# A recurrent and convolutional backbone on one core: the recurrence's GpSimd operations on VectorE

## The chip, the cores and the metric

The kernel runs on one core of a Trainium2 chip. The metric is the device time of one execution in microseconds; the time before is the median of three runs.

## The reference

A stream of 512 latent tokens of width 1024 with 256 context tokens goes through two layers. Layer 0 mixes the tokens with a gated linear recurrence in both directions (8 heads of 128 features, chunks of 64 steps), layer 1 with a short gated convolution; each is followed by a squared-ReLU MLP. All weights are fp32. What matters here is layer 0's recurrence:

```python
def step(s, blk):                       # one chunk of 64 steps
    qb, kb, vb, gb = blk
    cum = jnp.cumsum(gb, axis=2)        # g = log f, f the forget gate, k = 1 - f
    ref = cum[:, :, CHUNK // 2 - 1:CHUNK // 2]
    last = cum[:, :, -1:]
    o_inter = einsum('bhck,bhkv->bhcv', qb * exp(cum), s)
    scores = einsum('bhck,bhsk->bhcs', qb * exp(cum - ref), kb * exp(ref - cum))
    scores = where(lower, scores, 0.0)
    o_intra = einsum('bhcs,bhsv->bhcv', scores, vb)
    s_new = exp(last)[:, :, 0, :, None] * s + einsum('bhsk,bhsv->bhkv', kb * exp(last - cum), vb)
    return s_new, o_inter + o_intra
...
o = o * rsqrt(mean(o * o, axis=-1, keepdims=True) + EPS)      # per head
o = o * gnorm * silu(gate);  y = o.reshape(...) @ w_out
```

Context tokens give only the state from which each direction of the latent scan starts.

## The kernel before, in words

Features lie in partitions, tokens in the free dimension. Every fp32 product of weights and activations is made of three products of a high and a low part: ScalarE casts the high part (`whi`, L316), another engine subtracts it from the fp32 tile for the low part (`wlo`, L317; 128x1024 for half a block of weights). TensorE takes weights high with activations high and low first, and the remaining low part last (L340, L343).

Layer 0 runs head by head, in pairs (`hp`), an even head A and an odd head B. For a head, `logs` (L646) makes the sums of log f on VectorE: minimum (L666), two scans per direction (L671, L672; L678, L680), the difference to the chunk's middle (L685), then the context's part: `gc` (L694), its scan (L697), the keys k (L702), the chunk ends `el` (L705), the context's keys (L709), and at its end the decayed context keys `kc` (L711). ScalarE runs Ln and Exp between them. `latent_ops` (L740) then makes the operands of the latent products for each direction: three products of keys (`kl`, and both halves of d3, L750 to L753), the products with q (L755 to L760). TensorE transposes `kc` (`ctr`, L718), makes the context's state, transposes the keys (`ktr`, L778), and makes the states, the masked scores and the output.

TensorE's queue is in program order, and the order around the recurrence is written out by hand: `Fill` puts as many products of the next block between the recurrence's steps as the table `GAPS` says (for head 7: 30 ahead of `ctr`, 20 behind it). These products are the next head's forget gates (`forget_steps`, whose weights `wf` come in two halves, for heads 1 to 7) and queries, or in head 7 the out projection of heads 0 to 3 (`out_steps`). That one multiplies `y_hi` and `y_lo` of a finished head (`y_split`, L230); for heads 0 to 3 they are traced behind head 7's `latent_ops`, and `h_pair` gives them the slots of the input activations h0, which come free when the last products with h0 are done. `readout` (L829) scales a head's y with gain and gate, then with the reciprocal root (L833).

On the other engines the framework's scheduler sets the order: an engine takes, of the operations whose inputs are ready by the scheduler's reckoning, the one traced first; blocks under `tc.high_priority()` (the weights' parts among them) come ahead of the rest. Once built, each engine runs its queue strictly in order.

Of the kernel before, what the change touches and what calls it, by code (L numbers as in the profile page):

```python
# [13 lines left out]
ALU = mybir.AluOpType  # L14
PSUM = bass.MemoryType.PSUM
DRAM = bass.MemoryType.DRAM
# products between the steps of a head's recurrence: before and behind the context's transposes, behind those of each
# direction's keys (and before its second scores), before the output's products and before its mean square's
# [10 lines left out]
P = 128  # L29
# [17 lines left out]
def dit_kernel(ctx, tc, x, c, ctx_in, c_ctx, ada_w, ada_b, norm1, norm2, norm_f, mlp_w1, mlp_w2,  # L47
# [31 lines left out]
    # ScalarE's functions run in groups that one table set serves; the order of the groups is held.  # L79
# [19 lines left out]
    def dma_w(dst, src):  # L99
        """Weights in the order of their use; the vectors' loads come behind those traced so far."""  # L100
        ins = nc.sync.dma_start(dst, src)
        if weight_dma[0] is not None:
            tc.add_manual_dep(ins.ins, weight_dma[0].ins.name, NOSYNC, reason="load order")
        return ins
# [9 lines left out]
    # ---------------------------------------------------------------- loads of the set-up  # L114
# [12 lines left out]
    def ada_chunk(k):  # L127
        """Columns of feature tile k of the first shift (0..127) and scale (128..255), as two halves over the rows."""
# [27 lines left out]
    # ---------------------------------------------------------------- constants  # L156
# [7 lines left out]
    # adds rows 2, 3 of four to rows 0, 1  # L164
# [25 lines left out]
    # silu(c), silu(c_ctx); feature index p * KT + j  # L190
# [9 lines left out]
    # ---------------------------------------------------------------- norms  # L200
# [4 lines left out]
    def pin(*names):  # L205
        """The order of these operations on their engine."""
        for a, b in zip(names, names[1:]):
            tc.add_manual_dep(pins[b].ins, pins[a].ins.name, NOSYNC, reason="order")

    def rsqrt(v, w, name, n, pool=None):  # L210
        """1 / sqrt(v / n + EPS), with a Newton step behind the tables' values."""
# [14 lines left out]
    def split(t, c0, c1, shift, hi, lo, eng=nc.vector):  # L226
        """hi + lo = t + shift, hi with the bits that a float32r product carries."""
# [14 lines left out]
    # tokens in partitions: 1 / rms of each as a row, alike in all partitions  # L242
# [28 lines left out]
    def first_parts(k):  # L271
        """The parts of the weights' columns behind the shift and scale of feature tile k."""
        raws = ada_raw.get(k) or ada_chunk(k)
        with tc.high_priority():
            ada_parts[k] = [part for h in range(2) for part in split_first(raws[h], f"adst{k}_{h}")]

    def first_rows(k):
        """Rows (products with the parts of c, c_ctx) of the shift and scale of feature tile k."""
# [12 lines left out]
    # ------------------------------------------------- vectors as feature columns  # L291
# [19 lines left out]
    # ---------------------------------------------------------------- weights  # L311
# [8 lines left out]
    def load_half(name, *srcs, **kw):  # L320
        """KH * P rows by CB columns of weights as (hi, lo); the columns may come in pieces."""
# [6 lines left out]
    def load_block(name, *srcs, **kw):  # L328
        """D rows by CB columns, as two halves over the rows."""
        return [load_half(f"{name}_{h}", *(s[h * KH * P:(h + 1) * KH * P, :] for s in srcs), **kw) for h in range(2)]  # L330

    def mm_steps(ps, w, ms, rhs, ks, c0, c1, first, last, fresh=False):
        """The products of the k tiles ks (of one half) in W[:, ms].T @ (hi + lo)[:, c0:c1]; last those of the part
        that comes last: rhs's lo if it is `fresh`, the weights' lo otherwise."""
# [16 lines left out]
    def block_steps(w, pss, rhs):  # L351
        """Both feature tiles of a block, one product at a time."""
# [4 lines left out]
    class Fill:  # L357
        """Products that TensorE runs between the steps of a head's recurrence, while other engines work on these."""
# [4 lines left out]
        def gap(self):  # L363
            """The products that the next wait takes, behind what has come so far."""
# [6 lines left out]
        def step(self, first, last=None):  # L371
            """A step of the recurrence."""
# [4 lines left out]
        def finish(self, i=0):  # L377
            """The rest of the products of the i-th kind."""
# [6 lines left out]
    def block_products(w, rhs, consume, name, c0, c1, m=0, norm=None, parts=0, fresh=False):  # L385
        """Both feature tiles of a block, rows in halves outside. TensorE's part of a `norm` whose sums are still
        on their way comes behind `parts` of the block's products."""
        # a fresh operand's first block does not wait for the banks of the products before it
# [13 lines left out]
    def later(done, c0, c1):  # L402
        """A norm that is due once the products behind it are under way."""
# [3 lines left out]
    def stage(srcs, rhs, consume, name, first=0, last=0, done=None):  # L407
        """All blocks; the first `first` and the last `last` of them together, in halves of the columns.
        `done` is called with each half of the columns that the last blocks have finished."""
# [3 lines left out]
        for gi, g in enumerate(groups):  # L413
            halved = (first > 1 and gi == 0) or (last and gi == len(groups) - 1)
            # behind a norm, VectorE has the norm's work
# [11 lines left out]
    # ---------------------------------------------------------------- adaLN vectors  # L427
# [44 lines left out]
    def ada_finish(ins=None):  # L472
        """The columns of vectors whose rows have come back; behind ins, as the way through DRAM takes its time."""
# [28 lines left out]
    # ---------------------------------------------------------------- first adaLN vectors, h and hc  # L502
# [12 lines left out]
    def first_vectors(k):  # L515
        """shift and scale of feature tile k, for latent and context."""
# [29 lines left out]
    # the first two blocks take the feature tiles as they come  # L546
# [4 lines left out]
    def other_vectors():  # L551
# [5 lines left out]
        # lower bounds: softmax over the layer axis (size N), cumulative sum minus first  # L557
# [72 lines left out]
    # ---------------------------------------------------------------- layer 0: HGRN2  # L630
# [15 lines left out]
    def logs(zs, hd):  # L646
        """Sums of log f. zs: {"c": (z, sigmoid), 0: .., 1: ..}; the operations that ScalarE's Exp waits for first."""
# [14 lines left out]
        for d in range(2):  # L662
            r = R[d]
            z, g, gi, name = r["z"], r["g"], r["gi"], f"{hd}_{d}"
            # the table's logarithm ends at 2^-64; without a lower bound log f is z down there
# [26 lines left out]
        for d in range(2):  # L692
            zd = zc[:, d * CTX:(d + 1) * CTX]
            nc.vector.scalar_tensor_tensor(out=gs[d], in0=zd, scalar=col(lbig, d, hd), in1=gs[d], op0=ALU.add, op1=ALU.min)  # L694
            # the sums over the steps behind each one, one column on from the step's own
# [18 lines left out]
    def context_states(kc, hd, vc, fill):  # L714
        """Both directions' states behind the context; kc = (forward | backward) columns, decayed to the end."""
# [24 lines left out]
    def latent_ops(r, q, d, name):  # L740
        """Operands of the products over pairs of chunks; `f` is the pair's first chunk in this direction."""
# [8 lines left out]
        nc.gpsimd.tensor_tensor(out=v3(kl), in0=v4(kk)[:, :, f, :], in1=v4(d3)[:, :, f, :], op=ALU.mult)  # L750
        nc.gpsimd.tensor_tensor(out=v4(d3)[:, :, 1 - f, :], in0=v4(kk)[:, :, 1 - f, :], in1=v4(d3)[:, :, 1 - f, :],
                                op=ALU.mult)
        nc.gpsimd.tensor_tensor(out=v4(d3)[:, :, f, :], in0=v3(kl), in1=bc(1 - f), op=ALU.mult)  # L753
# [40 lines left out]
    def recurrence(hd, ops, s0, v, fill):  # L794
        """Masked scores, states and o (times QS) of a head; leaves o in yT and its mean square's sums in PSUM."""
# [18 lines left out]
        if hd < HEADS - 1:  # L814
            # the squares in two parts, as the weights are
# [13 lines left out]
    def readout(hd, pr, gate):  # L829
# [3 lines left out]
        (nc.gpsimd if hd < HEADS - 1 else nc.vector).tensor_tensor(out=y, in0=y, in1=r, op=ALU.mult)  # L833

    def silu_part(part, hp, qg):
        def f(m, ps, c0, c1):
            s = ht("qg", f"qg{part}_{hp}_{m}", SEQ, 4)
            act_fn(s, ps, AF.Sigmoid)
            # q, and with it every product up to o, is carried times QS: room for the scores behind the mask
# [5 lines left out]
    def forget_steps(hd, got):  # L845
        got["w"] = w = load_block(f"f{hd}", *fcols(hd), eng=nc.gpsimd)
# [16 lines left out]
    def out_steps():  # L863
        """The out projection of heads 0 .. 3."""
# [42 lines left out]
    for hp in range(4):  # L907
# [41 lines left out]
        if hp == 3:  # L949
            for hd in range(KH):  # L950
                y_split(hd, nc.gpsimd)
# [307 lines left out]
```

## Time and profile before

| | |
|---|---|
| median of 3 runs | 1451.79 us (1449.75 to 1454.37) |
| span of the profiled execution | 1450.0 us |
| TensorE busy | 1383.1 us (95%) |
| VectorE busy | 914.6 us (63%) |
| ScalarE busy | 578.8 us (40%) |
| GpSimd busy | 185.6 us (13%), 160 instructions |
| mean granted TensorE clock | 0.982 |

The recurrence of layer 0 lies between about 80 and 540 us. Engines in the rows: PE is TensorE's products, DVE VectorE, ACT ScalarE, POOL GpSimd. A product's "busy" is modelled, products overlap, and the time from one start to the next is what one costs. An engine's idle time before an instruction stands in brackets with what ended it.

### The profile page before, as it was taken

The page shows a single profiled execution, that of the slowest core. Times are in us where ns is not written, and L with a number is a line of the kernel's source. Part 1 is how long each engine was busy: PE and PEld are TensorE (multiplying, and loading weights), DVE is VectorE, ACT ScalarE, POOL GpSimd, SP SyncE. Part 2 cuts the span into 40 slices and gives each one's busy share as a digit, 9 for nine tenths or more (in the row PEclk, how much of TensorE's full clock was granted, in tenths as well). Part 3 has the DMA queues.
Part 4 walks back from the last instruction along what each step waited for, and adds up shares of the span by engine and source line. Part 5 has one row for each costly group of instructions (what it writes and reads, how often), then busy time and mean ns, then how long its engine had stood idle before and what let it go on. Part 6 is the DMA issues. An engine that isn't in the chain of part 4 may idle for free.

```text
span 1450.0 us, 18678 instructions
## 1 busy us (share of the span) xinstructions
PE 1383.1 (95%) x7418; PEld 1171.7 (81%) x7418; DVE 914.6 (63%) x1305; ACT 578.8 (40%) x877; POOL 185.6 (13%) x160
## 2 busy tenths in 40 slices
PE   6999899989899989999999999999999999999997
PEld 4797787878787779788888888988898788888887
DVE  6695876876776888666566446644467644444436
ACT  6573355445355444233242333322234423232333
POOL 3031232141132130000000003000030100000000
PEclk9999999999999999999999999999999999999999
DMA  9623213333221133775566332332324532332311
GB/s 267 200 59 102 88 45 102 116 93 97 59 74 44 59 131 131 232 218 164 182 190 191 116 92 74 98 102 88 102 91 156 160 102 87 102 102 87 102 58 59
DMA packets 142267, 167.60 MB, mean 116 GB/s; under 512 B 6692, under 2 KB 121572, under 8 KB 142180
## 3 DMA queue, kind: packets, MB, share of 16 engines
q1 hardware_dynamic: 140964, 164.70, 36.4%
q0 software_dynamic: 1088, 1.65, 0.5%
q8 instruction: 58, 0.95, 0.3%
q14 instruction: 29, 0.24, 0.0%
q10 hardware_dynamic: 128, 0.05, 0.0%
HBM read 164.25 MB, written 2.14 MB: 115 GB/s over the span
## 4 chain that ended last, share of the span: by engine, by line
PE 62%; DVE 11%; ACT 2%; DMA 2%; issue 1%; DVEq 0%; SPq 0%; ACTq 0%
PE ps_w L340 20%; PE ps_w L343 10%; PE ps_w2t L1197 4%; PE ps_w2t L1196 4%; PE ps_w2t L1198 4%; DMA ada<-in_ada_w_dram 2%; PE ps_cvb L340 2%; PE ps_cwo L340 2%; PE ps_cvc L340 2%; PE ps_cvx L340 2%; PE ps_fl L340 1%; PE ps_cvb L343 1%; DVE mt_a L1017 1%; PE ps_cwo L343 1%; DVE h_a_lo L233 1%
## 5 line engine op out<-in xcount | busy, mean ns | idle before, releaser
L316 ACT CAST whi_w<-raw_w 128x1024 fp32r<-128x1024 f32 x128 | 134.0, 1052 | 276.7 <-PE ps_w L340 145.5
L317 DVE TENSOR_TENSOR wlo_w<-raw_w,whi_w 128x1024 fp32r<-128x1024 f32 x116 | 141.4, 1222 | 160.5 <-ACT whi_w L316 159.9
L340 PE MATMUL ps_w<-h_a_hi,whi_w 128*128 128x512 f32 (+1 forms) x576 | 208.5, 368 | 2.5 <-ACT h_a_hi L232 2.5
L340 PE MATMUL ps_w<-h_a_lo,whi_w 128*128 128x512 f32 x448 | 174.4, 389 | 0.0
L340 PEld LDWEIGHTS ps_w<-h_a_hi,whi_w 128*128 128x128 f32 x576 | 109.2, 190 | 21.1 <-ACT h_a_hi L232 2.9
L444 DVE SCALAR_TENSOR_TENSOR acc<-ada,cs,acc 128x1024 f32<-128x1024 f32 x70 | 90.6, 1294 | 49.8 <-DMA ada<-in_ada_w_dram 49.7
L343 PE MATMUL ps_w<-h_a_hi,wlo_w 128*128 128x512 f32 x448 | 119.7, 389 | 0.0
L1196 PE MATMUL ps_w2t<-whi_w,u_hi 128*128 128x512 f32 (+1 forms) x288 | 105.4, 366 | 0.0
L1197 PE MATMUL ps_w2t<-wlo_w,u_hi 128*128 128x512 f32 (+1 forms) x288 | 105.4, 366 | 0.0
L1198 PE MATMUL ps_w2t<-whi_w,u_lo 128*128 128x512 f32 (+1 forms) x288 | 105.3, 366 | 0.0
L340 PE MATMUL ps_w<-u_lo,whi_w 128*128 128x512 f32 (+1 forms) x288 | 103.4, 366 | 0.4 <-DVE u_lo L1068 0.4
L340 PE MATMUL ps_w<-u_hi,whi_w 128*128 128x512 f32 (+1 forms) x288 | 103.5, 367 | 0.0
L343 PEld LDWEIGHTS ps_w<-h_a_hi,wlo_w 128*128 128x128 f32 x448 | 84.1, 188 | 17.5
L340 PEld LDWEIGHTS ps_w<-h_a_lo,whi_w 128*128 128x128 f32 x448 | 84.1, 188 | 17.3
L1067 DVE TENSOR_TENSOR mr<-mr 128x512 f32<-128x512 f32 (+1 forms) x72 | 45.0, 629 | 45.6 <-ACT u_hi L1066 45.6
L1065 ACT ACTIVATE mr<-ps_w 128x512 f32<-128x512 f32 (+1 forms) x72 | 39.2, 545 | 81.7 <-PE ps_w L343 81.6
L343 PE MATMUL ps_w<-u_hi,wlo_w 128*128 128x512 f32 (+1 forms) x288 | 70.2, 366 | 0.0
L340 PEld LDWEIGHTS ps_w<-u_lo,whi_w 128*128 128x128 f32 x288 | 54.4, 189 | 9.6 <-DVE u_lo L1068 0.8
L340 PEld LDWEIGHTS ps_w<-u_hi,whi_w 128*128 128x128 f32 x288 | 54.3, 189 | 9.1
L1198 PEld LDWEIGHTS ps_w2t<-whi_w,u_lo 128*128 128x128 f32 x288 | 54.4, 189 | 8.8 <-issue 0.2
L1196 PEld LDWEIGHTS ps_w2t<-whi_w,u_hi 128*128 128x128 f32 x288 | 54.4, 189 | 8.8
L1197 PEld LDWEIGHTS ps_w2t<-wlo_w,u_hi 128*128 128x128 f32 x288 | 54.4, 189 | 8.7
(376 smaller groups left out, 3245.2 us busy)
## 6 DMA issues: line engine op xcount, KB each, us to landing
raw_w<-in_mlp_w_dram SPq DMA_DIRECT2D x128, 512.0 KB, 3.8
ada<-in_ada_w_dram SPq DMA_DIRECT2D x80, 512.0 KB, 4.5
adaw<-in_ada_w_dram SPq DMA_DIRECT2D x32, 256.0 KB, 5.4
raw_f<-in_hgrn_w_in_dram SPq DMA_DIRECT2D x32, 256.0 KB, 3.5
raw_p<-in_hgrn_w_in_dram SPq DMA_DIRECT2D x12, 512.0 KB, 3.5
raw_v<-in_hgrn_w_in_dram SPq DMA_DIRECT2D x8, 512.0 KB, 4.7
raw_cvb<-in_conv_w_in_dram SPq DMA_DIRECT2D x8, 512.0 KB, 3.7
raw_cwo<-in_conv_w_out_dram SPq DMA_DIRECT2D x8, 512.0 KB, 3.5
```

The costliest lines, as they stand in the source:

```text
L233: i1 = nc.vector.scalar_tensor_tensor(out=lo[:, c0:c1], in0=t, scalar=shift, in1=hi[:, c0:c1], op0=ALU.add, op1=ALU.subtract)
L316: pins[name] = nc.scalar.copy(hi, raw)
L317: eng.tensor_tensor(out=lo, in0=raw, in1=hi, op=ALU.subtract)
L340: yield nc.tensor.matmul(ps, lhsT=w[i][:, k % KH, ms], rhs=rhs[k][j][:, c0:c1], start=(k == first and (i, j) == (0, 0)), stop=False)
L343: yield nc.tensor.matmul(ps, lhsT=w[late[0]][:, k % KH, ms], rhs=rhs[k][late[1]][:, c0:c1], start=False, stop=(k == last))
L444: ins = nc.vector.scalar_tensor_tensor(out=acc, in0=raw[:, 0, :], scalar=cs[:, j, 0:1], in1=acc, op0=ALU.mult, op1=ALU.add)
L1017: ins = nc.vector.scalar_tensor_tensor(out=t, in0=xT[k][:, c0:c1], scalar=a[:, k:k + 1], in1=r, op0=ALU.mult, op1=ALU.mult)
L1065: nc.scalar.activation(r, ps, AF.Relu)
L1067: nc.vector.tensor_tensor(out=r, in0=r, in1=r, op=ALU.mult)
L1196: nc.tensor.matmul(ps, lhsT=u[k][0][:, tk], rhs=whi[:, kk, c0:c1], start=(k == 0), stop=False)
L1197: nc.tensor.matmul(ps, lhsT=u[k][0][:, tk], rhs=wlo[:, kk, c0:c1], start=False, stop=False)
L1198: nc.tensor.matmul(ps, lhsT=u[k][1][:, tk], rhs=whi[:, kk, c0:c1], start=False, stop=(k == KT - 1))
```

## The change

Four groups of operations go from GpSimd to VectorE; nothing else changes (the diff also drops comments, which keeps the line numbers). The three key products of `latent_ops` (16 times each), the low parts of the forget weights (two halves for each of heads 1 to 7), the last scaling of y in the readouts of heads 0 to 6, and the low parts of y for heads 0 to 3 (`y_split` without an engine uses VectorE). `GAPS` stays as it is.

```diff
-        nc.gpsimd.tensor_tensor(out=v3(kl), in0=v4(kk)[:, :, f, :], in1=v4(d3)[:, :, f, :], op=ALU.mult)
-        nc.gpsimd.tensor_tensor(out=v4(d3)[:, :, 1 - f, :], in0=v4(kk)[:, :, 1 - f, :], in1=v4(d3)[:, :, 1 - f, :],
+        nc.vector.tensor_tensor(out=v3(kl), in0=v4(kk)[:, :, f, :], in1=v4(d3)[:, :, f, :], op=ALU.mult)
+        nc.vector.tensor_tensor(out=v4(d3)[:, :, 1 - f, :], in0=v4(kk)[:, :, 1 - f, :], in1=v4(d3)[:, :, 1 - f, :],
                                 op=ALU.mult)
-        nc.gpsimd.tensor_tensor(out=v4(d3)[:, :, f, :], in0=v3(kl), in1=bc(1 - f), op=ALU.mult)
+        nc.vector.tensor_tensor(out=v4(d3)[:, :, f, :], in0=v3(kl), in1=bc(1 - f), op=ALU.mult)
...
-        (nc.gpsimd if hd < HEADS - 1 else nc.vector).tensor_tensor(out=y, in0=y, in1=r, op=ALU.mult)
+        nc.vector.tensor_tensor(out=y, in0=y, in1=r, op=ALU.mult)
...
-        got["w"] = w = load_block(f"f{hd}", *fcols(hd), eng=nc.gpsimd)
+        got["w"] = w = load_block(f"f{hd}", *fcols(hd))
...
-                y_split(hd, nc.gpsimd)
+                y_split(hd)
```

## Rows read from the trace of the kernel before

**Rows 1.** Stretches: busy us (count) of PE, PEld, DVE, ACT, POOL; PEclk; DMA.
```profile
80.00:540.00 460.00, 422.08 (x2594) 363.92 (x2594) 344.50 (x510) 219.86 (x346) 127.10 (x106) 0.96 0.28 84
...
155.40:162.20 6.80, 4.71 (x13) 3.90 (x14) 6.80 (x15) 1.29 (x3) 0.10 (x1) 0.50 0.26 77
250.90:254.30 3.40, 2.79 (x7) 1.64 (x6) 3.40 (x7) 2.83 (x4) 2.35 (x3) 0.50 0.36 107
...
363.60:370.40 6.80, 4.12 (x12) 3.45 (x13) 6.80 (x15) 3.79 (x5) 2.48 (x5) 0.50 0.28 80
```

**Rows 2.** Waits of PE, 80 to 540 us: total us, times, longest.
```profile
PE ctr L718 <- DVE kc L711: 12.4, 7, 5.2
...
PE ps_p L340 <- DVE gc L694: 3.1, 1, 3.1
PE ps_woa L343 <- POOL y_lo L230: 3.0, 3, 1.7
...
PE psv L890 <- DVE gc L694: 1.5, 2, 1.3
...
PE ps_fl L340 <- DVE gc L694: 1.1, 1, 1.1
```

**Rows 3.** Timeline of PE, heads 1, 3, 5: start, us, instruction, idle before.
```profile
157.49 1.12 PE L718 MATMUL ctr<-ident,kc 128*128 128x128 f32 x4 [4.27 <-DVE kc L711]
...
254.73 0.66 PE L718 MATMUL ctr<-ident,kc 128*128 128x128 f32 x4 [1.03 <-DVE kc L711]
...
366.28 1.12 PE L718 MATMUL ctr<-ident,kc 128*128 128x128 f32 x4 [5.23 <-DVE kc L711]
```

**Rows 4.** Timeline of DVE, heads 3 and 4.
```profile
242.37 0.67 DVE L685 TENSOR_TENSOR zb<-c 128x512 f32<-128x512 f32 x1
...
246.61 2.87 DVE L697 TENSOR_TENSOR_SCAN gc<-ones,gc 128x255 f32<-128x255 f32 x1
...
249.78 0.15 DVE L705 COPY el<-c 128x8 f32<-128x8 f32 x1
...
302.33 0.68 DVE L697 TENSOR_TENSOR_SCAN gc<-ones,gc 128x255 f32<-128x255 f32 x1
```

**Rows 5.** POOL: one instruction, then its group by line (busy us, mean ns).
```profile
246.11 2.83 POOL L317 TENSOR_TENSOR wlo_f<-raw_f,whi_f 128x1024 fp32r<-128x1024 f32 x1
...
L317 POOL TENSOR_TENSOR wlo_f<-raw_f,whi_f 128x1024 fp32r<-128x1024 f32 x14 | 36.9, 2638 | 118.9 <-ACT whi_f L316 114.0 <-PE ps_p L343 3.7 <-ACT qg L110 1.2
```

**Rows 6.** Groups of DVE by line and shape, 80 to 540 us.
```profile
L685 DVE TENSOR_TENSOR zb<-c 128x512 f32<-128x512 f32 x16 | 16.7, 1044 | 0.0
...
L697 DVE TENSOR_TENSOR_SCAN gc<-ones,gc 128x255 f32<-128x255 f32 x16 | 14.9, 933 | 0.0
L317 DVE TENSOR_TENSOR wlo_p<-raw_p,whi_p 128x1024 fp32r<-128x1024 f32 x12 | 14.7, 1221 | 17.6 <-ACT whi_p L316 17.6
L709 DVE TENSOR_SCALAR kc<-kc,lb1n,lb 128x256 f32<-128x256 f32 x16 | 12.3, 803 | 0.0
...
L705 DVE COPY el<-c 128x8 f32<-128x8 f32 x16 | 7.5, 466 | 0.0
L755 DVE TENSOR_TENSOR e<-el 128x4 f32<-128x4 f32 x16 | 7.3, 456 | 0.0
...
L759 DVE TENSOR_TENSOR c<-qg,c 128x256 f32<-128x256 f32 x16 | 6.6, 411 | 0.0
```

**Rows 7.** Timeline of ACT, head 4: the readout's Exp.
```profile
295.15 0.63 ACT L110 ACTIVATE y_o<-y_o 128x512 f32<-128x512 f32 x1
```

**Rows 8.** Timeline of DVE: head 4's readout; head 7's last latent product.
```profile
312.77 0.67 DVE L220 TENSOR_SCALAR nt_o<-oms 128x512 f32<-128x512 f32 x1
...
483.75 0.41 DVE L760 TENSOR_TENSOR c<-ql,el 128x256 f32<-128x256 f32 x1
```

**Rows 9.** Timeline of PE, head 7: out projection and context transposes.
```profile
465.65 0.39 PE L340 MATMUL ps_woa<-y_hi,wlo_woa 128*128 128x512 f32 x1
465.88 0.39 PE L343 MATMUL ps_woa<-y_lo,whi_woa 128*128 128x512 f32 x1
...
478.77 0.60 PE L718 MATMUL ctr<-ident,kc 128*128 128x128 f32 x4
```

## The prediction

> **What bounds the kernel now.** I read the granted clock and the busy shares by stretch first, then TensorE's waits, then the timelines of the engines around those waits, then the groups by line. The edits lie in the recurrence, 80 to 540 us. There TensorE is busy 422.1 of 460 us, VectorE 344.5 and GpSimd 127.1 [rows 1]: TensorE is the bound, and only 38 us of its idle time, with what the lowered clock costs it, can be won. So the question is which of its waits the moved work ends or makes. The waits [rows 2]: 12.4 us for `kc` (L711), 3.1, 1.1 and 1.5 us for `gc` (L694, which frees a PSUM bank), 3.0 us for `y_lo`. Both `kc` and `gc` end one VectorE chain: from `g` (L666) through the scans to `kc`, once per head. In heads 1 and 5 `kc` is late by 4.27 and 5.23 us [rows 3]; in the even heads by about half a microsecond.
>
> VectorE is late there partly because of GpSimd. A scan of 128x255 (L697) takes 0.68 us by itself and took 2.87 us from 246.61 [rows 4], while GpSimd's `wlo_f` subtraction ran from 246.11 to 248.94 [rows 5]: it ended 0.54 us behind it. The copy of 128x8 (L705) takes 0.15 us, the subtraction of 128x512 (L685) 0.67 us [rows 4], but over the 16 of each the means are 0.47 and 1.04 us, L697's 0.93 and the 128x4 product's (L755) 0.46 [rows 6]. L709's 128x256 pass means 0.80, where another 128x256 operation, L759, takes 0.41.
>
> [...]
>
> **The change part by part.** (1) Stalls leave VectorE's chain. Per head ahead of `kc`, from the means less the undisturbed durations: L685 2 x 0.37, L697 2 x 0.25, L705 2 x 0.32, L709 2 x 0.39 (0.41 as its own price is an estimate from L759), L755 once 0.31: 2.97 us on average, 23.8 over eight heads. In heads 1, 3 and 5 a whole `wlo_f` falls into the chain; at 2.87 - 0.68 = 2.19 us each that is 6.6. The rest, 17.2, is 2.1 per head. So an even head's chain loses 2.1 us and that of heads 1, 3, 5 loses 4.3.
>
> (2) Fourteen `wlo_f` (128x1024) come to VectorE, two halves for each of seven heads. On GpSimd one takes 2.64 us [rows 5]; on VectorE the twin `wlo_p` takes 1.22 [rows 6], 17.1 in all. They are traced at high priority, so I let one of a head's two stand ahead of `kc`: 1.2 us. The other falls into VectorE's idle time ahead of the chain or behind `kc`.
>
> (3) Forty-eight key products (128x256). L759 has their shape [rows 6]: 0.41 us, 19.7 us in all, 2.5 per head. They are traced behind the logs. Where VectorE waits for ScalarE's Exp ahead of `kc`, L755 and L756, a 128x4 and a 128x512 product, already fill the hole; two key products can take their place. I take nothing ahead of `kc`, and 2.5 us as the other end. Behind `kc` they are covered: the key transposes that need them stand in TensorE's queue behind `ctr`, filling products and the context's states.
>
> (4) Seven last scalings of y (128x512, 0.67 us as L685) stand behind the rsqrt and ahead of the state updates: between 0, where VectorE has time, and 7 x 0.67 = 4.7 us. TensorE is not among those that wait for long behind a readout now, so I take 1.0 in all.
>
> (5) Four `y_lo` (0.67 us each) in head 7. This one costs. An operation traced later is not let into the chain: L220 of a readout had its input from ScalarE at 295.78 and ran on VectorE at 312.77, behind the last latent product [rows 7, 8]. `y_lo` is traced behind both directions' latent products too, and its input comes only with the chain under way, as y takes h0's slots. TensorE's queue holds 30 out-projection products ahead of the context transposes `ctr`; the ninth, at 465.88, needs the first `y_lo`. VectorE's last latent product ran at 483.75 [rows 8]. It ends at 484.2; less 4.3 us of stalls, or twice that as the four `y_lo` on GpSimd hold head 7's chain too, plus 2.5 of key products, it ends at 478 to 482.4. Four `y_lo` bring 481 to 485, and the 18 products left of the 30, at 0.23 us from start to start [rows 9], put `ctr` at 485 to 489 instead of 478.77: 6 to 10 us later. I take 7, near the lower end, as the stalls by `y_lo` are sure. The 3.0 us for `y_lo` are swallowed by this.
>
> What TensorE gets: heads 1, 3, 5 each 4.3 - 1.2 = 3.1 us (their waits are 5.4, 4.1 and 5.2, so it all counts): 9.3. The four even heads each 2.1 - 1.2 = 0.9 against waits of (12.4 - 4.27 - 5.23 - 1.03 + 1.5) / 4, about 0.85 (head 3's own wait for `kc` is 1.03): 3.0 taken. Of the 5.8 us of clock, half, as part of the waits stays: 2.9; ends 0 and 5.8. Sum: 9.3 + 3.0 + 2.9 - 1.0 - 7.0 = 7.2 us. What is late next is `kc` again in heads 1 and 5, by about 2 us, and `y_lo` in head 7. No SyncE queue is passed; GpSimd's queue loses the operations that stood ahead of its memsets and small DMAs, which no row shows TensorE waiting for, so nothing for that, and less than 1 us if it did.
>
> [...] The row: L697 was held until GpSimd's subtraction was through [rows 4, 5]. [...]
>
> **The rivals.** First: `y_lo` finds a hole in VectorE's chain (an operation that waits for its own predecessor leaves one) and the chain gains more than the means show. For it: GpSimd's first `y_lo` input was ready early in the chain, and TensorE's own waits are all on VectorE. Against it: row 312.77. Then head 7 loses nothing and wins its 3.0, the three odd heads win 5.4 + 4.1 + 5.2 = 14.7 less 2 x 1.2 that stays, with the even heads' 3.0 and the clock's whole 5.8: about 21 us, 1431.
>
> Second, slower: the key products are put ahead of `kc`. Place: between L697 and L711 in every head; price: six at 0.41, 2.5 us of chain, against 2.1 that the even heads' stalls give back and 1.2 for `wlo_f`. From 0.9 us of insertion on, TensorE waits longer than now in an even head. Then heads 1, 3, 5 win 0.6 each, the even heads lose 1.6 each, the clock gives nothing, head 7 costs 7 and the readouts 1: 1.8 - 6.4 - 8 = 12.6 us slower, 1464; with half of them ahead, 1458. For it: those products are ready while the chain still runs. Against it: they are traced behind the logs, and later-traced work is seen to stay out.
>
> Third: the chain gains, but TensorE's products and the PSUM banks take over, and head 7's hole eats all: within 2 us of 1452. For it: TensorE is 92% busy here already. Against it: the named waits are whole stops, at the end of a chain that gets shorter.
>
> **How the numbers follow.** The profiled execution spans 1450.0 us, the median of the runs is 1451.8, 0.12% more; the sum is made on the former and taken from the latter: 1451.8 - 7.2 = 1444.6. Its own ends: clock 0 and head 7 at 10 give 1.3 us (1450.5); clock 5.8 and head 7 at 6 give 11.1 (1440.7). Chances: forecast 0.45, first rival 0.18, second 0.20, third 0.17. The range, 1431 to 1459, leaves out the second rival's far half and half of the first. 0.3% is 4.4 us, about what can be told from no change: faster takes 0.8 of the forecast and the first rival, 0.54; the same gets the rest of the forecast and most of the third, 0.24; slower 0.22.
>
> **What would show it.** In the profile after: L697, L705, L709 and L755 at their undisturbed durations; GpSimd's busy time in the recurrence down by far more than `wlo_f`'s 36.9 us while VectorE's stays within 10 of 344.5 (17.1 + 19.7 + 7.4 come, 23.8 and the stalls behind `kc` go); TensorE's wait for `kc` under 5 us in sum and no half clock behind head 3; one wait of 10 us or more for `y_lo`, now from VectorE, with the clock low behind it. It would be wrong if key products stand ahead of L711, if `wlo_f` waits on VectorE for its ScalarE half with the chain queued behind it, or if `y_lo` runs before the latent products.

## The result, and the profile after

The changed kernel takes 1431.13 us (median of 5 runs, 1429.17 to 1434.27) against 1449.75 us of the kernel before in the same series: a ratio of 0.9869, 95% interval 0.9852 to 0.9886. It is 18.6 us faster; 7.2 us were forecast. The direction holds, and the range by 0.1 us; the size does not. Ratios here are estimated from all runs of a series, so they are not the quotients of the two medians and can differ from them by up to 0.2%. The profiled execution spans 1428.6 us (1450.0 before) at a mean granted clock of 0.990 (0.982).

The page's first part after the change, busy time and number of instructions of each engine:

```profile
PE 1372.0 (96%) x7418; PEld 1165.9 (82%) x7418; DVE 911.0 (64%) x1378; ACT 578.6 (40%) x877; POOL 79.0 (6%) x87
```

VectorE has 73 instructions more and is busy 3.6 us less than before (914.6 us). The 14 `wlo_f` at 1.22 us, the 48 key products at 0.42, seven scalings of y at 0.69 and four `y_lo` at 0.65 make 44.9 us of new work. So stalls have left VectorE: 48.5 us by its busy time, in which instructions that overlap count once, and 39.5 us when the durations of the operations that both kernels have there are added up. Either is far above the 23.8 that the forecast counted ahead of `kc`.

The groups of VectorE by line and shape, 80 to 530 us (busy us, mean ns), answer [rows 6]:

```profile
L317 DVE TENSOR_TENSOR wlo_f<-raw_f,whi_f 128x1024 fp32r<-128x1024 f32 x14 | 17.1, 1221 | 0.4 <-ACT whi_f L316 0.4
L697 DVE TENSOR_TENSOR_SCAN gc<-ones,gc 128x255 f32<-128x255 f32 x16 | 11.0, 685 | 0.0
L685 DVE TENSOR_TENSOR zb<-c 128x512 f32<-128x512 f32 x16 | 10.8, 672 | 0.0
L758 DVE TENSOR_TENSOR ql<-qg,c 128x256 f32<-128x256 f32 x16 | 6.8, 424 | 0.0
L750 DVE TENSOR_TENSOR kl<-k,g 128x256 f32<-128x256 f32 x16 | 6.8, 422 | 0.0
L709 DVE TENSOR_SCALAR kc<-kc,lb1n,lb 128x256 f32<-128x256 f32 x16 | 5.9, 412 | 0.0
L755 DVE TENSOR_TENSOR e<-el 128x4 f32<-128x4 f32 x16 | 2.6, 161 | 0.0
L705 DVE COPY el<-c 128x8 f32<-128x8 f32 x16 | 2.5, 158 | 0.0
```

Each of the five stalled lines has the undisturbed duration that was taken for it. L758, a latent product behind `kc`, was in no sum; before it read:

```profile
L758 DVE TENSOR_TENSOR ql<-qg,c 128x256 f32<-128x256 f32 x16 | 15.5, 969 | 0.0
```

8.7 us of stalls have gone from this line alone, all of it behind `kc`.

TensorE's waits after, 80 to 540 us (total us, times, longest), answer [rows 2]:

```profile
PE ps_woa L343 <- DVE y_lo L230: 12.4, 1, 12.4
PE ctr L718 <- DVE kc L711: 5.4, 3, 2.0
PE adaps L461 <- DVE alo L455: 2.9, 1, 2.9
...
PE sc L768 <- DVE S L789: 1.8, 1, 1.8
...
PE psv L890 <- DVE gc L694: 0.8, 1, 0.8
```

Three rows of the same view before, which the forecast left out:

```profile
PE adaps L461 <- DVE alo L455: 6.2, 1, 6.2
PE kv L784 <- DVE S L789: 2.3, 2, 1.2
PE sc L768 <- DVE scm L772: 1.6, 1, 1.6
```

The stretches at half clock before, beside those of [rows 1] (columns as there):

```profile
117.80:124.60 6.80, 6.80 (x20) 5.16 (x19) 4.42 (x7) 0.00 (x0) 0.00 (x0) 0.50 0.11 43
315.80:322.60 6.80, 5.79 (x16) 4.12 (x17) 2.85 (x3) 2.37 (x4) 3.65 (x4) 0.50 0.16 45
469.40:476.20 6.80, 5.77 (x13) 4.13 (x13) 6.80 (x11) 4.34 (x7) 5.02 (x5) 0.50 0.10 22
```

And after, the recurrence and all its stretches at half clock:

```profile
80.00:540.00 460.00, 430.20 (x2740) 376.24 (x2739) 360.17 (x623) 232.15 (x373) 23.41 (x33) 0.98 0.27 84
300.60:304.00 3.40, 3.40 (x10) 2.64 (x9) 3.05 (x4) 1.73 (x4) 0.61 (x2) 0.50 0.12 29
344.90:348.30 3.40, 3.40 (x10) 2.63 (x10) 3.40 (x11) 3.37 (x5) 0.00 (x0) 0.51 0.07 20
443.90:457.60 13.70, 3.97 (x8) 2.65 (x9) 13.47 (x32) 5.92 (x9) 0.00 (x0) 0.50 0.12 38
```

Before, TensorE worked 30.0 us at a granted clock of 0.50, after 10.8 (0.50 to 0.51). In the trace before, a 128x512 product took 0.43 us from start to start at 0.50 (120.06 to 123.05 us) and 0.23 at 1.00 (124.71 to 125.86). The account takes half of the busy time at the lower clock as lost, an estimate from the granted 0.50: 15.0 and 5.4 us. By 0.43 and 0.23 it would be 14.0 and 5.0.

**The account.** The mean square's product `ms_a` (L998) is the first operation behind the recurrence's last products. The table splits the time from 80 us to its start into TensorE's named waits (without the one of 2.4 to 2.5 us right ahead of `ms_a`, which every kernel has), what the half clock costs (by that estimate half of the time that TensorE was busy at it), and the rest, for the profiled execution of every kernel told of below.

| kernel | ms_a starts | waits | half clock | rest |
|---|---|---|---|---|
| before | 528.3 | 34.0 | 15.0 | 399.3 |
| changed | 510.4 | 26.1 | 5.4 | 398.9 |
| changed, another execution (e11) | 513.1 | 26.6 | 6.8 | 399.7 |
| before + key products (e1) | 520.0 | 30.1 | 12.8 | 397.1 |
| before + forget low parts (e2) | 520.9 | 28.7 | 13.5 | 398.7 |
| before + both (e8) | 505.5 | 18.0 | 9.8 | 397.7 |
| before + second halves of heads 1, 3, 5, 7 (e10) | 523.4 | 30.0 | 14.6 | 398.8 |
| changed, y_lo back (e3) | 504.1 | 18.5 | 8.5 | 397.1 |
| changed, y_lo first (e4) | 506.1 | 19.9 | 8.5 | 397.7 |
| y_lo first and more products (e9) | 498.7 | 18.3 | 1.7 | 398.7 |
| changed + GpSimd reads (e5) | 534.9 | 43.0 | 11.6 | 400.3 |
| changed + GpSimd writes (e6) | 508.3 | 26.6 | 5.3 | 396.4 |
| changed, other fillers in head 7 (e7) | 506.9 | 21.0 | 9.8 | 396.1 |

The rest stays within 396.1 to 400.3 us, so waits and half clock carry most of the differences. From `ms_a` to the end, where nothing was edited, all these executions take 918 to 923 us.

### The profile page after: what moved, and what is told of

It is laid out like the page before. It is cut to its first block, busy times and chain, and to the rows that moved or that the text cites. A ratio compares the mean times of both kernels' runs of the same rounds, so it can differ in the third digit from the quotient of the medians.

```text
span 1428.6 us, 18668 instructions
## 1 busy us (share of the span) xinstructions
PE 1372.0 (96%) x7418; PEld 1165.9 (82%) x7418; DVE 911.0 (64%) x1378; ACT 578.6 (40%) x877; POOL 79.0 (6%) x87
## 4 chain that ended last, share of the span: by engine, by line
PE 74%; DVE 16%; DMA 3%; ACT 3%; issue 2%; SPq 0%; POOL 0%; DVEq 0%; ACTq 0%
PE ps_w L340 20%; PE ps_w L343 10%; PE ps_w2t L1197 4%; PE ps_w2t L1198 4%; PE ps_w2t L1196 4%; PE ps_fl L340 3%; DMA ada<-in_ada_w_dram 3%; PE ps_cvb L340 2%; PE ps_cwo L340 2%; PE ps_cvx L340 2%; PE ps_cvc L340 2%; PE ps_fl L343 2%; PE ps_fc L340 2%; PE sc L768 1%; PE ps_p L340 1%
## 5 line engine op out<-in xcount | busy, mean ns | idle before, releaser
L340 PEld LDWEIGHTS ps_w<-h_a_hi,whi_w 128*128 128x128 f32 x576 | 108.6, 189 | 21.1 <-ACT h_a_hi L232 2.8
```

Source lines behind the costliest of these rows:

```text
L340: yield nc.tensor.matmul(ps, lhsT=w[i][:, k % KH, ms], rhs=rhs[k][j][:, c0:c1], start=(k == first and (i, j) == (0, 0)), stop=False)
```

## The experiments

**e1: the key products alone.** The kernel before with one part of the change:

```diff
-        nc.gpsimd.tensor_tensor(out=v3(kl), in0=v4(kk)[:, :, f, :], in1=v4(d3)[:, :, f, :], op=ALU.mult)
-        nc.gpsimd.tensor_tensor(out=v4(d3)[:, :, 1 - f, :], in0=v4(kk)[:, :, 1 - f, :], in1=v4(d3)[:, :, 1 - f, :],
+        nc.vector.tensor_tensor(out=v3(kl), in0=v4(kk)[:, :, f, :], in1=v4(d3)[:, :, f, :], op=ALU.mult)
+        nc.vector.tensor_tensor(out=v4(d3)[:, :, 1 - f, :], in0=v4(kk)[:, :, 1 - f, :], in1=v4(d3)[:, :, 1 - f, :],
...
-        nc.gpsimd.tensor_tensor(out=v4(d3)[:, :, f, :], in0=v3(kl), in1=bc(1 - f), op=ALU.mult)
+        nc.vector.tensor_tensor(out=v4(d3)[:, :, f, :], in0=v3(kl), in1=bc(1 - f), op=ALU.mult)
```

Expected: 

> The kernel before with the three key products alone on VectorE (forget weights' low parts, y's scaling and y_lo stay on GpSimd). Theory 1 (GpSimd's operations held VectorE's chain): the short stalls at L705, L709, L755 and L685 go, about 2.1 us per head, so the waits for kc shrink by some 6 us in heads 1, 3, 5 and by 3 in the even heads, with some clock back: 1434 to 1440 us. Theory 2 (the gain comes from forget weights that are ready sooner): no more than 2 us of change, 1448 or above. Theory 3 (the key products put ahead of kc cost what the stalls give back): 1446 to 1455.

Measured: 1441.82 us against 1450.39, ratio 0.9944 (0.993 to 0.9959), 8.6 us faster: less than the 1434 to 1440 us of theory 1, and in none of the three stretches. One group of VectorE and one of GpSimd, 80 to 530 us:

```profile
L755 DVE TENSOR_TENSOR e<-el 128x4 f32<-128x4 f32 x16 | 13.7, 854 | 0.0
...
L317 POOL TENSOR_TENSOR wlo_f<-raw_f,whi_f 128x1024 fp32r<-128x1024 f32 x14 | 48.6, 3472 | 155.0 <-ACT whi_f L316 151.1 <-PE ps_p L343 3.7
```

Part of the stalls went: L697's mean fell from 933 to 683 ns, L685's from 1044 to 737. Part of them moved: the small product L755 now takes 0.85 us (0.46 before, 0.16 after), and `wlo_f` on GpSimd 3.47 instead of 2.64 [rows 5] with VectorE's products beside it. TensorE's waits fall by 3.9 us only. Those behind `kc` grow: `sc` for `scm` 4.5 us (1.6 before), `kv` for `S` 4.3 (2.3).

**e2: the forget weights' low parts alone.** The kernel before with:

```diff
-        got["w"] = w = load_block(f"f{hd}", *fcols(hd), eng=nc.gpsimd)
+        got["w"] = w = load_block(f"f{hd}", *fcols(hd))
```

Expected: 

> The kernel before with the forget weights' low parts alone on VectorE. Theory 1: only the 2.2 us stalls by a whole low part go, in heads 1, 3 and 5, against 1.2 us of the operation itself in each head: 1444 to 1450 us. Theory 2 (forget weights ready sooner): most of the 18.6 us, 1438 or below. Theory 3 has nothing to say here, 1450.

Measured: 1442.78 us, ratio 0.9953 (0.9937 to 0.997), 7.6 us faster, more than the part ahead of `kc` explains, and far from the 1438 us or less that theory 2, forget weights that are ready sooner, had asked for. TensorE's wait for `kc` grew, 14.4 us in seven waits, longest 4.2: the key products are still on GpSimd, and the chain there is still held (L685 takes 935 ns on average, L709 832). Behind `kc` it is quiet:

```profile
L758 DVE TENSOR_TENSOR ql<-qg,c 128x256 f32<-128x256 f32 x16 | 6.6, 412 | 0.0
```

L758 is undisturbed, the wait for `alo` fell from 6.2 to 3.6 us, and the half clock behind it, at 315.8, is gone. From head 4's `ctr` to head 5's it is 53.2 us instead of 59.5. That was the first sign that the stalls behind `kc` reach TensorE.

**e8: both together.** The edits of e1 and e2 on one kernel (of the key products one stands here); y's last scaling and `y_lo` stay on GpSimd.

```diff
-        nc.gpsimd.tensor_tensor(out=v3(kl), in0=v4(kk)[:, :, f, :], in1=v4(d3)[:, :, f, :], op=ALU.mult)
+        nc.vector.tensor_tensor(out=v3(kl), in0=v4(kk)[:, :, f, :], in1=v4(d3)[:, :, f, :], op=ALU.mult)
...
-        got["w"] = w = load_block(f"f{hd}", *fcols(hd), eng=nc.gpsimd)
+        got["w"] = w = load_block(f"f{hd}", *fcols(hd))
```

Expected: 

> The kernel before with the key products and the forget weights' low parts on VectorE; y's last scaling and the four low parts of y stay on GpSimd. Against the run with y_lo alone on GpSimd (1427.8 us) it shows the price of the seven scalings on VectorE. As predicted they cost 1 us: 1425 to 1428. If they gain, as the state updates no longer meet GpSimd: 1428 to 1431. Theory 1 asks for more than the sum of the two parts run alone (8.6 and 7.6 us), as only without both is the chain free in the odd heads: at least 20 us under the kernel before.

Measured: 1427.45 us against 1450.92, ratio 0.9838 (0.9822 to 0.9854). That is 23.5 us, where the single parts add up to 16.2. The account shows where: the waits fall by 3.9 (e1), 5.3 (e2) and 16.0 us (e8). The stalls do add up: over the operations that both kernels have on VectorE they fall by 17, 20 and 37 us, against 20, 17 and 37 us of work that comes. But each part alone leaves operations ahead of `kc` held (means of 854 ns on L755 in e1, 935 on L685 and 832 on L709 in e2; 154, 737 and 406 with both). That this is why the waits do not add up is argued from these means; that the gains of the parts are less than that of both is measured.

**e3: y_lo back on GpSimd.** The changed kernel with:

```diff
-                y_split(hd)
+                y_split(hd, nc.gpsimd)
```

Expected: 

> The changed kernel with the four low parts of y for heads 0 to 3 back on GpSimd, so that only they are left there in head 7. Theory 1 with the hole in head 7 as told (ctr 7 us late in that head): the wait of 12.4 us for y_lo goes, ctr of head 7 comes 6 to 9 us sooner though the four hold VectorE's chain again, 1422 to 1426 us. If the hole costs nothing because VectorE's chain would have ended late anyway: 1429 to 1433.

Measured: 1427.79 us, ratio to before 0.9834 (0.9816 to 0.9853), against 0.9869 (0.9852 to 0.9886) of the whole change: `y_lo` on VectorE costs 0.35%, 5.1 us, less than the 1422 to 1426 us of theory 1 asked for; the two intervals just touch. The 12.4 us hole is gone, and `ms_a` starts 6.3 us earlier (504.1 for 510.4). e3 and e8 differ in the readouts' scaling alone: 0.9834 and 0.9838. So moving y's scaling cost nothing that these intervals, 0.2% (3 us) to either side, can show.

**e4: y_lo on VectorE, but first.** The changed kernel with:

```diff
-            for hd in range(KH):
-                y_split(hd)
+            with tc.high_priority():
+                for hd in range(KH):
+                    y_split(hd)
```

Expected: 

> The changed kernel with the same four low parts on VectorE but at high priority, so that they run inside head 7's chain, about 2.4 us ahead of kc, as soon as their high parts are there. Theory 1: TensorE's 12.4 us wait goes, kc is 2.4 us later than in the changed kernel but still in time, ctr of head 7 comes about 12 us sooner, and the clock does not fall there: 1417 to 1421 us. If the delay of kc by 2.4 us reaches TensorE: 1421 to 1424. If the hole cost nothing: 1431 or more.

Measured: 1426.39 us, ratio 0.9835 (0.9817 to 0.9853); better than the change by about 5 us, but no better than e3 and not at the time expected. Head 7's `ctr` comes 11.1 us sooner behind head 6's (49.99 us for 61.11), but from there to `ms_a` it takes 53.7 us instead of 49.6. What is late next stands in VectorE's queue: the readout of the head before now lies among the state updates `S`:

```profile
465.52 0.68 DVE L220 TENSOR_SCALAR nt_o<-oms 128x512 f32<-128x512 f32 x1
466.12 0.34 DVE L789 SCALAR_TENSOR_TENSOR S<-S,e,kv 128x128 f32<-128x128 f32 x1
466.37 0.69 DVE L221 TENSOR_TENSOR nt_o<-nt_o,y_o 128x512 f32<-128x512 f32 x1
466.98 0.34 DVE L789 SCALAR_TENSOR_TENSOR S<-S,e,kv 128x128 f32<-128x128 f32 x1
```

TensorE waits 1.83 us for `S` at 468.23, and behind it the granted clock is 0.50 (471.0 to 472.7 us):

```profile
468.23 0.49 PE L768 MATMUL sc<-e,zb 128*128 128x128 f32 x2 [1.83 <-DVE S L789]
```

**e5 and e6: which work on GpSimd holds VectorE.** The changed kernel with work on GpSimd that nobody uses, written to a scratch tile, in each direction's `latent_ops`. e5 reads operands, as the key products did; e6 writes almost alone, behind one narrow product that sets its time.

```diff
+        sg, mg = scr_g.rearrange("p (n t) -> p n t", t=64), v3(mz[:, 0:128])
+        for i in range(4):
+            nc.gpsimd.tensor_tensor(out=sg, in0=v4(kk)[:, 0:2, i % 2, :], in1=mg, op=ALU.mult)
+        for i in range(2):
+            nc.gpsimd.tensor_tensor(out=sg, in0=mg, in1=el4[:, 0:2, i:i + 1].broadcast_to([P, 2, 64]), op=ALU.mult)
```

Expected of e5: 

> The changed kernel with extra work on GpSimd that nobody waits for: per head and direction four products of 128x128 that read the keys k (ready early in VectorE's chain) and two that read the chunk ends el, all written to a scratch tile. The result is untouched. Theory 1 (GpSimd's reading holds VectorE's chain): the stalls come back, L697, L705, L709 and L755 at 1.2 to 3 times their undisturbed means, kc 1.5 us late in each head, 1435 to 1443 us. Rival (the gain came from the operations being quicker and in better order on VectorE, the stalls are not its cause): 1429 to 1433 us, as the changed kernel.

```diff
+        for src, n in ((kk, 12), (el, 6)):
+            nc.gpsimd.tensor_tensor(out=scr_g[:, 0:1], in0=src[:, 0:1], in1=one1, op=ALU.mult)
+            for i in range(n):
+                nc.gpsimd.memset(scr_g, 0.0)
```

Expected of e6: 

> As the run with extra reading, but GpSimd's extra work only writes: a one-column product sets the moment (behind k and behind el), then 18 memsets of 128x128 on the scratch tile per direction, about as long in all. If any busy GpSimd holds VectorE: 1435 to 1443 us, with the same stalls. If only its reading does for instructions with two inputs from SBUF: stalls at L705 and L709 at most, which have one input, 1430 to 1435 us.

Measured: e5 1454.56 us, ratio to before 1.0025 (1.0012 to 1.0037), the whole gain gone and a little more, which is far above the 1435 to 1443 us expected; e6 1430.09 us, 0.9868 (0.9843 to 0.9892), the change's own time. Engine totals of e5's page, then groups of its GpSimd and VectorE, 80 to 530 us (its lines from 633 on stand one to six further down):

```profile
PE 1380.5 (95%) x7418; PEld 1171.0 (80%) x7418; DVE 932.1 (64%) x1378; ACT 578.9 (40%) x877; POOL 166.2 (11%) x183
```

```profile
L757 POOL TENSOR_TENSOR scr_g<-k,mz 128x128 bf16<-128x128 f32 x64 | 60.7, 948 | 159.5 <-DVE k L703 155.2
...
L712 DVE TENSOR_TENSOR kc<-kc,gc 128x512 f32<-128x512 f32 x8 | 7.3, 909 | 0.0
```

The same of e6:

```profile
PE 1370.7 (96%) x7418; PEld 1163.6 (81%) x7418; DVE 913.0 (64%) x1378; ACT 578.9 (41%) x877; POOL 168.8 (12%) x407
```

```profile
L758 POOL MEMSET scr_g<- 128x128 bf16 x288 | 59.9, 208 | 16.2
...
L712 DVE TENSOR_TENSOR kc<-kc,gc 128x512 f32<-128x512 f32 x8 | 5.4, 680 | 0.0
```

GpSimd is busy as long in both, 166.2 and 168.8 us (87 and 90 more than in the changed kernel), and VectorE has the same 1378 instructions. With reads beside it, VectorE's busy time rises by 21.1 us (911.0 to 932.1), and the kernel's by 23.4; with writes beside it neither moves by more than 2. So here work on GpSimd that reads cost the kernel time through VectorE, though nobody needs its results. That the old placement's price was of this kind, and not GpSimd's slowness, is argued from it and from the waits before the change: the only one of TensorE for GpSimd was `y_lo`'s 3.0 us [rows 2]. L712, a product of two tiles, took 909 ns on average beside reads and 680 beside writes.

**e7: other fillers in head 7.** The changed kernel with head 7's `GAPS` so that `ctr` does not stand behind the products that need `y_lo`:

```diff
-        (30, 20, 4, 6, 4, 18, 7))
+        (8, 0, 0, 30, 20, 24, 7))
```

Expected: 

> The changed kernel with another row of GAPS for head 7: 8, 0, 0, 30, 20, 24, 7 in place of 30, 20, 4, 6, 4, 18, 7, so that the products that need y_lo stand behind the states' first steps and not ahead of ctr. Theory (the hole is the order of the products against y_lo): TensorE no longer waits 12.4 us, but some 3 us for ScalarE between ctr and the states; ctr of head 7 comes about 14 us sooner, the head's output 7 to 9 us sooner: 1422 to 1426 us. If VectorE's states and masks, now without that pause, become late instead, half of it is given back: 1426 to 1430.

Measured: 1433.61 us, ratio 0.9883 (0.9867 to 0.99): a miss, no better than the change. The wait for `y_lo` is gone, and with it the products that had covered the wait for `kc`:

```profile
444.06 1.11 PE L718 MATMUL ctr<-ident,kc 128*128 128x128 f32 x4 [4.33 <-DVE kc L711]
446.76 2.08 PE L727 MATMUL cst<-vc,kcT 128*128 128x128 f32 x8 [1.59 <-ACT kcT L723]
```

And the clock takes the rest. The stretch behind these waits:

```profile
441.90:459.00 17.10, 12.79 (x46) 10.14 (x47) 13.10 (x31) 8.23 (x13) 0.00 (x0) 0.50 0.10 32
```

12.8 us of work at half clock cost 6.4 by the account's half, where the changed kernel's long hole had only 4.0 us of work in its half-clock stretch (6.8 in e11). Here the long wait with little to do behind it was cheaper at the clock than short ones with work between them.

**e10: stalls behind kc alone.** The kernel before, with only the second half of `wlo_f` of heads 1, 3, 5 and 7 on VectorE. That half runs on GpSimd behind `kc`, so the chain ahead of `kc` keeps its stalls:

```diff
-        got["w"] = w = load_block(f"f{hd}", *fcols(hd), eng=nc.gpsimd)
+        got["w"] = w = [load_half(f"f{hd}_{h}", *(s[h * KH * P:(h + 1) * KH * P, :] for s in fcols(hd)),
+                                  eng=nc.vector if hd % 2 and h else nc.gpsimd) for h in range(2)]
```

Expected: 

> The kernel before with four operations moved: the second half's low part of the forget weights that are loaded in the even heads (heads 1, 3, 5, 7), which on GpSimd run behind kc and hold VectorE's latent products (L758, 2.65 us in place of 0.41). The prediction counted such stalls behind kc at nothing: 1449 to 1452 us. If they reach TensorE through the state updates and head 4's adaLN products: their waits shrink by 1 us per head and head 4's half clock goes or shortens, 1444 to 1448 us.

Measured: 1446.91 us against 1451.91, ratio 0.9976 (0.9963 to 0.9989): 3.5 us for four operations. TensorE's waits in the recurrence:

```profile
PE ctr L718 <- DVE kc L711: 11.4, 7, 5.2
PE adaps L461 <- DVE alo L455: 3.6, 1, 3.6
```

The wait for `kc` is almost what it was (12.4 us in [rows 2]), its longest the same 5.2. The wait for `alo` fell by 2.6 us, that of `kv` for `S` is gone (a wait of `sc` for `S` of 2.7 us stands where `sc` waited 1.6 us for `scm`), and L758's mean fell from 969 to 414 ns. The stalls behind `kc` cost TensorE time, and 3.5 us (1.6 to 5.4 by the interval) is the price of these four by themselves.

**e9: more products where the waits are.** e4 with more filling products ahead of `ctr` in heads 1, 3 and 5:

```diff
-        (66, 9, 5, 6, 4, 6, 0),
+        (74, 9, 5, 4, 2, 2, 0),
...
-        (22, 20, 10, 6, 4, 14, 18),
+        (28, 20, 8, 4, 4, 12, 18),
...
-        (18, 24, 5, 10, 6, 19, 14),
+        (27, 24, 5, 8, 4, 14, 14),
```

Expected: 

> The kernel with y_lo at high priority, and with more products ahead of ctr in heads 1, 3 and 5 (74, 28 and 27 in place of 66, 22 and 18), taken from the later gaps of the same heads. What is late next by the trace of the changed kernel is kc, by 2.0, 1.3 and 2.0 us in these heads: 8, 6 and 9 products at 0.23 us fill that. If the later gaps have cover to spare: 5 us and some clock less than y_lo first's 1426.4, 1418 to 1423 us. If the later steps then wait in their place: 1424 to 1430.

Measured: 1420.87 us against 1451.91, ratio 0.9805 (0.9784 to 0.9826), the fastest here, ahead of both kernels (its interval overlaps e4's). The waits for `kc` fall from 5.4 to 0.2 us, but by the account all waits together are only 1.6 us less than in e4; the half clock, at 1.7 us instead of 8.5, is most of the gain. The fillers taken from the later steps open a new wait, for `qg`; that for `S` (4.3 us in e4) is not new, nor are the 3.3 us for `xT` that both have:

```profile
PE ps_fl L340 <- DVE qg L840: 4.1, 2, 2.6
PE sc L768 <- DVE S L789: 4.0, 3, 1.8
```

**e11: the changed kernel again**, beside e9 and e10.

Expected: 

> The changed kernel as it is, on the same chip as the run with more products ahead, to price the hole in head 7 and the later steps against it: 1429 to 1434 us as before; with a hole of 7 to 10 us it stands 5 to 12 us above the run with more products ahead.

Measured: 1434.19 us against 1451.91, ratio 0.9892 (0.9867 to 0.9916). That is just above what was expected, and 13.3 us above e9, a little more than the 5 to 12 expected. The interval overlaps that of the first series; by the two ratios the change is worth 16 to 19 us.

## Why the prediction was right or wrong

**What bounds the kernel** was read rightly: TensorE, by its waits for VectorE and the clock behind them. The 21.4 us between the two profiled executions are 17.9 up to `ms_a` and 3.5 behind it, where nothing was edited and executions differ by as much.

**Stalls ahead of kc (step 1): right for those that it counts.** Of the waits for `kc` and `gc`, heads 1, 3 and 5 won 8.9 us (9.3 forecast), the even heads 2.6 (3.0).

**wlo_f on VectorE (step 2): right.** 1.22 us each, one of them ahead of `kc` in the odd heads. VectorE's timeline in head 5:

```profile
340.83 1.23 DVE L317 TENSOR_TENSOR wlo_f<-raw_f,whi_f 128x1024 fp32r<-128x1024 f32 x1
...
343.27 0.42 DVE L750 TENSOR_TENSOR kl<-k,g 128x256 f32<-128x256 f32 x1
343.60 0.69 DVE L711 TENSOR_TENSOR kc<-kc,gc 128x512 f32<-128x512 f32 x1
```

**Key products (step 3): one of six stands ahead of L711**, the `kl` at 343.27, where none was taken; in heads 2, 4 and 6 it is two. From start to start one costs a third of a microsecond, so this is 0.3 to 0.7 us per head, far from the second rival's 2.5. The `wlo_f` above it, 1.2 us, is as long as most of the wait for `kc` that is left in such a head (2.0 us in heads 1 and 5).

**Readouts (step 4): a cost of 1.0 was taken, none is seen**; e3 and e8 agree within their intervals, which are too wide to tell 1.0 us from nothing. The wait of `kv` for `S`, 2.3 us before, is gone; those of `sc` grew from 1.6 us (for `scm`) to 2.2 (1.8 for `S`, 0.4 for `scm`).

**Head 7 (step 5): right in mechanism, and a little smaller than its range of 6 to 10 us.** The operations behind head 7's latent products, and TensorE behind them:

```profile
451.34 0.43 DVE L760 TENSOR_TENSOR c<-ql,el 128x256 f32<-128x256 f32 x1
451.68 1.29 DVE L840 SCALAR_TENSOR_TENSOR qg<-qg,ps_p 128x512 f32<-128x512 f32 x2
452.87 1.30 DVE L230 TENSOR_TENSOR y_lo<-yT,y_hi 128x512 fp32r<-128x512 f32 x2
```

```profile
453.63 2.60 PE L343 MATMUL ps_woa<-y_lo,whi_woa 128*128 128x512 f32 x4 [12.37 <-DVE y_lo L230]
...
460.87 0.60 PE L718 MATMUL ctr<-ident,kc 128*128 128x128 f32 x4
```

`y_lo` stands behind the last latent product, as [rows 8] had suggested, TensorE waits 12.4 us, and `ctr` comes 5.4 us later behind head 6's than before (61.11 us for 55.68; 7 were taken). e3 gives 5.1 us for the whole kernel; in head 7 itself its `ctr` comes 9.4 us sooner (51.67 us behind head 6's), and two half-clock spells in heads 0 and 1, which the changed kernel's executions did not have, take 3.4 us back.

**The step that failed** is what step 1, and the sum made from it, leave out: stalls are counted "per head ahead of `kc`" and priced only in TensorE's waits that end there. Those behind `kc`, of which the prediction's last paragraph itself says that they go, have no term in the sum and no reason for having none; they were put at nothing. ("Behind `kc` they are covered", in step 3, is said of the key products, not of these stalls.) Behind `kc` stand the latent products, then the state updates, the readout and `alo`, and TensorE waits for some of these. In head 4 before:

```profile
307.24 2.65 DVE L758 TENSOR_TENSOR ql<-qg,c 128x256 f32<-128x256 f32 x1
...
315.54 1.22 DVE L455 TENSOR_TENSOR alo<-acc,ahi 128x1024 fp32r<-128x1024 f32 x1
```

```profile
316.81 0.59 PE L461 MATMUL adaps<-alo,one_r 128*1 128x512 f32 x1 [6.19 <-DVE alo L455]
```

The wait for `alo` gave 3.3 us, that of `kv` for `S` 2.3, less 0.6 at `sc`, and e10 shows 3.5 us for such stalls alone. The row that said so was in view: a wait of 6.2 us for `alo`, the second in size before the change and the longest single one, which the forecast left out.

The term for the clock failed by about as much. No run shows the 5.8 us of clock in the sum as a time of its own: in the three short stretches of [rows 1] TensorE was busy 11.6 us at a granted 0.50, which loses 5.4 us by 0.43 and 0.23 us for a product, and 5.8 by the account's half. Three half-clock spells were counted, those behind `kc` in heads 1, 3 and 5, and of their 5.8 us half; after the change 1.7 of it is left, so they gave 4.1 where 2.9 were taken. There were two more ahead of head 7, which no term held: at 117.8 behind a wait for `scm` and at 315.8 behind `alo`. They cost 6.3 us, and after the change one of 1.7 is left behind `alo`. So the clock gave 8.7 us in all. But 3.4 of it, the spell at 117.8, is not explained by shorter waits: the wait ahead of it was 1.6 us before and is 1.8 in the changed kernel, at full clock.

The whole sum reads: 8.9 + 2.6 + 8.7 + 2.3 + 3.3, less 0.6 at `sc` and 5.4 in head 7, is 19.8 against 17.9 seen at `ms_a`. Of the difference 1.1 us is counted twice (the wait of `kv` in head 6, at 434.12 before, lies in head 7's 55.68 us as well); 0.8 us is not placed. By the account the 17.9 us are 7.9 of waits, 9.6 of half clock and 0.4 of the rest.

**The first rival** gave the right time, 1431, by the wrong sum: it wanted `y_lo` in a hole of the chain, which did not come, and the odd heads' waits whole, of which 1.3 to 2.0 us each stay. Its half that was right is the clock's return. Nor do its own terms give 1431: 12.3 + 3.0 + 5.8 and head 7's 3.0 are 24.1 us, not about 21. (Likewise the second rival's half: with 1.25 us of key products per head ahead of `kc`, its prices give 3.9 us slower, 1456 and not 1458.) That the result lies in the range at all is luck: its lower end, 1431, is this rival's time and not the sum's.

**The signs named ahead:** GpSimd's busy time in the recurrence fell by 103.7 us (127.1 to 23.4); no half clock stands behind head 3; the long wait for `y_lo` came, with half clock from 443.9 to 457.6. The wait for `kc` is 5.4 us, just above the 5 that were named. One sign of being wrong came too: key products stand ahead of L711. VectorE's 360.2 us between 80 and 540 is not within 10 of 344.5, but more of the kernel falls into that stretch now; from 80 us to the start of `ms_a` it is 331.9 us for 333.6.

**What stays open:** whether a wait of about 2 us lowers the clock. In the changed kernel the waits of 1.8 us at 116.5 and 2.0 at 151.2 were followed by full clock, as 2.1 us each in e6 were; in e3, e4 and e8 waits of 2.0 to 2.6 us at the same places were followed by half clock, and in the kernel before one of 1.6 us was. Longer waits at full clock occur too: 2.4 us at 114.75 in e7, 3.3 us at 440.72 in e9. That is worth 3 to 5 us between executions of nearly the same queues, e9's small clock loss may owe something to it, and no run here settles what decides it.

## What to carry to other kernels

When work leaves GpSimd, price not only its duration but every VectorE line that it holds (here 87 us of reads on GpSimd added 21 us to VectorE's busy time), and follow each such line to the TensorE wait it ends in, those behind the obvious chain too. Count every half-clock spell that stands behind a VectorE wait, not only those of the chain that you mean to shorten; whether a spell goes with its wait the waits here do not foretell. An operation traced late on a busy engine can end up behind that engine's whole queue, as `y_lo` did here (TensorE waited 12.4 us for it): give it priority, then look for what it was hiding.

## What the runs showed of the hardware

**Reads held, writes did not.** 87 us of added GpSimd work that reads two operands cost VectorE 21 us of stalls; 90 us with 288 memsets cost it 2. The operation with a scalar L710 ran beside memsets all 16 times and took its 408 ns. Of the copy L706 only one of 16 lay beside them for more than a tenth of a microsecond, and that one took 0.29 us where the others took 0.14 to 0.17: one case, which settles nothing. So no run shows the stalls of operations with one input that the expectation of e6 allowed.

**The hold went both ways.** In e6 the one narrow product behind `el` took 1.22 us on average, the same product behind `k` 0.66, the shortest 0.31. One that began at 96.78 ended at 97.67, with VectorE's scan L698 (97.00 to 97.68). So VectorE's instructions seem to have kept GpSimd waiting in turn.

```profile
L756 POOL TENSOR_TENSOR scr_g<-el,ones 128x1 bf16<-128x1 f32 x16 | 19.5, 1221 | 31.7 <-DVE el L706 31.0
L756 POOL TENSOR_TENSOR scr_g<-k,ones 128x1 bf16<-128x1 f32 x16 | 10.6, 663 | 149.2 <-DVE k L703 148.6
```

**By the account's half, what the half clock cost is the work done in it, not its length.** The changed kernel's 12.4 us wait brought 13.7 us at half clock but only 4.0 us of work in it, 2.0 us lost; in e11 the same wait brought 17.1 us with 6.8 of work, 3.4 lost; e7's waits of 4.3 and 1.6 us brought 17.1 us with 12.8 of work, 6.4 lost.
